# Token-layout projections of two mixers in chunks of 512 columns, both token tiles in turn

## Chip, cores and metric

The kernel runs as one program on one core of a Trainium2 chip. The metric is the device time of the execution in microseconds (us). The kernel before has a median of 2323.62 us over 3 runs, from 2319.12 to 2325.05. Engines are named as the profile names them: PE is the matrix engine (its weight loads are PEld), DVE, ACT and POOL are the vector, scalar and GpSimd engines, and SP is the one that issues most of the DMA transfers.

## What is computed

A sequence of 256 tokens with 1024 features, in float32, goes through two transformer blocks of two layers each. Both have a SwiGLU feed-forward network (FFN), a token mixer and a second FFN per layer. The change touches one product in each mixer: the projection of the tokens whose result is wanted with tokens on the partitions (`z = h @ w_in` and `proj = n @ w_in` below).

```
# first block, per layer
h = rms_norm(x, mix_norm[l])
z = h @ w_in[l]                      # 1024 -> 3200
rq, rk, rv, rg, mq, mk, mv, ca, cg = split(z)
rq, rk = rotary(rq), rotary(rk)      # all 64 dims of a head
y_ret  = retention(rq, rk, rv)       # 6 heads, decay instead of softmax
y_ret  = silu(rg) * y_ret * rsqrt(mean(y_ret * y_ret) + EPS)
mq, mk = rotary(mq), rotary(mk)      # 16 of 64 dims
y_moba = moba_attention(mq, mk, mv)  # 6 heads; at 256 tokens causal attention
y_conv = conv_module(ca, cg, ...)    # 31 taps over time, layer norm, silu
x = x + concat(y_ret, y_moba, y_conv) @ w_out[l]

# second block, per layer
proj = n @ w_in
nsa_q, nsa_kv, nsa_g, dil_qkv, fox_qkv, fox_f, merge_g = split(proj)
y_a = nsa_attention(...)             # 4 heads; compressed, selected, windowed
y_b = dilated_attention(...)         # 3 groups of 2 heads, 3 patterns
y_c = forgetting_attention(...)      # 6 heads
g_a, g_b, g_c = split(sigmoid(merge_g))
merged = g_a * (y_a @ br_nsa) + g_b * (y_b @ br_dil) + g_c * (y_c @ br_fox)
h = h + ga2 * (merged @ w_out)
```

## The kernel before

**Stages.** The program is one straight list: FFN, `mixer1`, FFN for each of the two layers of the first block, then FFN, `mixer2`, FFN for each of the second. Python code emits instructions; a scheduler that simulates a timeline then chooses, at compile time, the order in which each engine gets them, and moves independent matmuls into places where another chain waits. So each engine runs a fixed list, in order, and waits where a value is not there yet.

**Products in three terms.** Every large product splits its float32 operands in a high and a low part. `weights` (L117) loads the weights in parts of 1024 columns (`raw`, 4 buffers, by SP); ACT casts the high part `whi` (L132) and DVE subtracts the low part `wlo` (L133), 5 buffers each. `mm3` (L152) issues three matmuls for one k-slice of 128 features: high by high, high by low, low by high (L155 to L157).

**The token projections.** `tok_proj` (L365) makes a chunk of n columns for both tiles of 128 tokens. The normalized activations `hh` and `hl` stand still in PE and the weights move. Its result `tp` holds both token tiles, 2 x n float32, in one PSUM bank of the tag `mm`, which has three; the second tile comes after the whole first. Mixer 1 has 9 chunks of 256 columns (36 heads of 64: retention q, k, v, then moba q, k, v). Mixer 2 has 12: 210, 192 and ten of 256.

**Rotations and copies.** ACT copies a chunk from PSUM to `tk` (in mixer 1 once for each token tile, scaled by `rt`; in mixer 2 once for both tiles, L964). `rope` (L376) then rotates up to four heads: for each token tile four DVE instructions (L391 to L394), with the scratch tiles `ra` and `rb` in two buffers of four heads.

**Mixer 1.** `heads(i)` (L618) is one chunk with its copies and rotations. The order as written: chunks 0 to 2, the transposes of retention's q and k (`pairs`, tile `tpo`, L405), the two inputs of the convolution (`conv_in`, L541, matmuls into `pc`), chunks 3 and 4, retention, chunks 5 to 7, transposes for moba, chunk 8, moba's attention. Retention takes two heads at a time: scores `sp`, on DVE the product with the decay (`pts`, L656), the product with v (`acc`, L451 and L453), a copy, a square, and its mean `st` (L580). The convolution's 31 taps of the first 128 channels run on DVE (L562); those of the other 128 on ACT (L566) and POOL (L567).

**Mixer 2.** Chunk 1 gives the compressed branch its keys and values; its hidden layer `phd` (L866) multiplies with weights that a DMA brings into `w1`. Chunks 2 and 3 give NSA its windowed keys and its queries; `pcm` (L909) is the first score of the compressed branch. Then follow NSA's attention, the dilated branch (L961 to L994: scores `sp`, masks into `smd`, a softmax over 384 and 768 columns, transposed probabilities `pt`, products `acc`), the forgetting attention ("fox") and the output. Beside them `merge_gate` (L801) makes the gates: 24 `pg` per layer, which depend on the input alone, so that the scheduler has them as free work for PE; 7 of them come ahead of the mixer's input. A gate needs one of the three `mm` banks, one of 2 `z` and one of 10 `gate` buffers, and a `gate` buffer comes free when `branch` has used it. The first NSA `branch` needs NSA's result.

## Time and profile before

| | |
|---|---|
| median of 3 runs | 2323.62 us |
| lowest, highest | 2319.12, 2325.05 us |
| the profiled execution's own time | 2322.81 us |
| its span | 2321.0 us |
| mean granted clock of PE | 0.987 |
| PE busy | 2250.6 us, 97% |
| PEld busy | 2113.9 us, 91% |
| DVE busy | 1762.8 us, 76% |
| ACT busy | 1207.3 us, 52% |

The shares are means over the whole span. Matmuls overlap one another in PE's pipeline, so the time from the start of one to the start of the next, not the duration of one, is what a matmul costs in a dense stream. The table by stretch gives busy time and, in brackets, the number of instructions of each engine between two times; the clock there is the share of full speed granted to PE. A row of the timeline has the start, the duration of the instruction (or of several alike, with their count), the engine, the line of the program, and what it writes and reads; in brackets at the end the idle time of the engine before it and what released it.

### The profile page before, as it was taken

To read this page: it belongs to the slowest core of one execution; us is meant where nothing else is said; L and a number is where in the kernel's file an instruction comes from. 1 tells how busy PE (TensorE), PEld (TensorE's weight loads), DVE (VectorE), ACT (ScalarE), POOL (GpSimd) and SP (SyncE) were. 2 spreads that over 40 slices of the span, in tenths; PEclk is the share of its full clock that TensorE was granted. 3 is DMA by queue.
4 is the path that set the end of the run, shared out by engine and by line. 5 is a ranking of instruction groups with operands and counts; after the bars stand their busy time and mean duration, and the time that the engine had idled before them with its cause. 6 is when DMAs were issued, how large, how long until landed. Compare 5 with 4: busy or idle time off the path is not lost.

```text
span 2321.0 us, 43297 instructions
## 1 busy us (share of the span) xinstructions
PE 2250.6 (97%) x16976; PEld 2113.9 (91%) x16976; DVE 1762.8 (76%) x3255; ACT 1207.3 (52%) x1939; POOL 271.7 (12%) x286
## 2 busy tenths in 40 slices
PE   8999899989989899999999999999999999999998
PEld 8989779979988879998998989999999999899997
DVE  8988868887877968877776667777677666678764
ACT  5545565445435655455555555555455555556543
POOL 2210511111110402111001000200000010011000
PEclk9999999999999989999999999999999999999999
DMA  8887327887888426875456644455655665335553
GB/s 289 306 287 283 122 97 275 292 301 245 293 280 274 141 90 227 285 238 188 172 177 198 199 121 121 132 199 182 184 191 182 179 204 182 101 110 187 186 177 114
DMA packets 121148, 464.79 MB, mean 200 GB/s; under 512 B 13744, under 2 KB 15408, under 8 KB 111472
## 3 DMA queue, kind: packets, MB, share of 16 engines
q1 hardware_dynamic: 119216, 454.43, 59.4%
q0 software_dynamic: 1728, 7.60, 0.9%
q8 instruction: 133, 2.18, 0.4%
q14 instruction: 71, 0.58, 0.1%
HBM read 460.93 MB, written 1.05 MB: 199 GB/s over the span
## 4 chain that ended last, share of the span: by engine, by line
PE 65%; DMA 13%; DVE 11%; issue 8%; ACT 1%; POOL 1%; DVEq 0%; SPq 0%; ACTq 0%; POOLq 0%
PE acc L163 12%; DMA adar<-in_ada 10%; PE acc L164 6%; PE at L266 4%; PE at L264 4%; PE at L265 4%; PE mm L266 4%; PE mm L264 4%; PE mm L265 4%; DVE wlo L133 4%; DVE adar L760 3%; PE tp L156 2%; PE tp L155 2%; PE tp L157 2%; PE pg L266 2%
## 5 line engine op out<-in xcount | busy, mean ns | idle before, releaser
L132 ACT CAST whi<-raw 128x1024 fp32r<-128x1024 f32 (+2 forms) x739 | 753.4, 1023 | 697.5 <-PE acc L163 146.1
L133 DVE TENSOR_TENSOR wlo<-raw,whi 128x1024 fp32r<-128x1024 f32 (+2 forms) x739 | 889.7, 1208 | 226.3 <-ACT whi L132 223.7
L163 PE MATMUL acc<-hid,whi 128*128 128x512 f32 x1408 | 494.3, 395 | 7.7 <-DVE hid L147 5.8
L264 PE MATMUL mm<-hh,whi 128*128 128x256 f32 (+1 forms) x1408 | 398.3, 283 | 9.4 <-ACT whi L132 4.9
L266 PE MATMUL at<-hh,wlo 128*128 128x256 f32 (+1 forms) x1408 | 398.1, 283 | 9.1 <-DVE wlo L133 9.0
L266 PE MATMUL mm<-hh,wlo 128*128 128x256 f32 (+1 forms) x1408 | 398.9, 283 | 4.3 <-DVE wlo L133 4.3
L264 PE MATMUL at<-hh,whi 128*128 128x256 f32 (+1 forms) x1408 | 397.7, 282 | 1.6 <-DVE p L347 1.6
L164 PE MATMUL acc<-hid,wlo 128*128 128x256 f32 x1408 | 395.8, 281 | 3.2 <-DVE wlo L133 3.2
L265 PE MATMUL mm<-hl,whi 128*128 128x256 f32 x1408 | 395.6, 281 | 0.4 <-DVE hl L187 0.4
L265 PE MATMUL at<-hl,whi 128*128 128x256 f32 x1408 | 395.5, 281 | 0.0
L163 PEld LDWEIGHTS acc<-hid,whi 128*128 128x128 f32 x1408 | 266.3, 189 | 68.0 <-DVE hid L147 7.0
L266 PEld LDWEIGHTS at<-hh,wlo 128*128 128x128 f32 x1408 | 266.2, 189 | 11.0 <-DVE wlo L133 10.8
L264 PEld LDWEIGHTS mm<-hh,whi 128*128 128x128 f32 x1408 | 266.4, 189 | 10.1 <-ACT whi L132 4.9
L266 PEld LDWEIGHTS mm<-hh,wlo 128*128 128x128 f32 x1408 | 267.0, 190 | 5.5 <-DVE wlo L133 5.3
L164 PEld LDWEIGHTS acc<-hid,wlo 128*128 128x128 f32 x1408 | 266.6, 189 | 4.0 <-DVE wlo L133 3.9
L265 PEld LDWEIGHTS mm<-hl,whi 128*128 128x128 f32 x1408 | 267.6, 190 | 1.8 <-DVE hl L187 1.5
L264 PEld LDWEIGHTS at<-hh,whi 128*128 128x128 f32 x1408 | 265.7, 189 | 2.2 <-DVE p L347 2.0
L265 PEld LDWEIGHTS at<-hl,whi 128*128 128x128 f32 x1408 | 267.3, 190 | 0.2
L760 DVE SCALAR_TENSOR_TENSOR adar<-adar,cb 128x1024 f32<-128x1024 f32 x144 | 177.0, 1264 | 78.2 <-DMA adar<-in_ada 77.8
L200 POOL TENSOR_TENSOR ssq<-ssq,sq 128x256 f32<-128x256 f32 x78 | 74.2, 954 | 930.6 <-ACT sq L198 919.8
L346 POOL TENSOR_TENSOR s<-s,rs 128x256 f32<-128x256 f32 x88 | 103.6, 1178 | 445.4 <-ACT s L345 442.1
L146 ACT CAST hid<-p 128x256 fp32r<-128x256 f32 x176 | 71.5, 406 | 103.5 <-DVE p L347 92.9
(373 smaller groups left out, 3943.7 us busy)
## 6 DMA issues: line engine op xcount, KB each, us to landing
raw<-in_g_in SPq DMA_DIRECT2D x176, 512.0 KB, 4.4
raw<-in_f_in SPq DMA_DIRECT2D x175, 512.0 KB, 5.9
adar<-in_ada SPq DMA_DIRECT2D x72, 1024.0 KB, 5.9
raw<-in_m_tok SPq DMA_DIRECT2D x76, 512.0 KB, 4.1
raw<-in_f_out SPq DMA_DIRECT2D x64, 512.0 KB, 5.3
raw<-in_g_out SPq DMA_DIRECT2D x64, 512.0 KB, 3.5
raw<-in_m_merge SPq DMA_DIRECT2D x48, 512.0 KB, 3.6
raw<-in_m_out SPq DMA_DIRECT2D x32, 512.0 KB, 3.4
```

The source lines that it names most:

```text
L132: nc.scalar.copy(hi[:, c], raw[:, c])
L133: nc.vector.tensor_sub(lo[:, c], raw[:, c], hi[:, c].bitcast(F32))
L146: nc.scalar.copy(hi, src)
L155: mm(out, a[0], b[0], start=first, stop=False)
L163: mm(out, a[0], b, start=first, stop=False, skip_group_check=True)
L164: mm(out[:, 0], a[1], b[:, 1], start=False, stop=last, skip_group_check=True)
L200: nc.gpsimd.tensor_tensor(ssq, ssq, sq, op=ALU.add)
L264: mm(out, w[0], self.hh[:, k, 0:n], start=k == 0, stop=False)
L265: mm(out[:, 0:S], w[0], self.hl[:, k], start=False, stop=False)
L266: mm(out, w[1], self.hh[:, k, 0:n], start=False, stop=k == KD - 1)
L346: nc.gpsimd.tensor_tensor(s, s, rs, op=ALU.mult)
L760: nc.vector.scalar_tensor_tensor(raw[:, e], raw[:, e], 1.0, self.cb, op0=ALU.mult, op1=ALU.mult, accum_out=self.mod[:, l, j + e:j + e + 1])
```

## The change

**Chunks.** `tok_proj` with more than 256 columns now takes two tiles of 128 x n, one for each token tile, each a whole bank of `mm`; so a chunk holds two of the three banks. The loop over k is outside and the token tiles are inside, so that the three matmuls of one tile are followed by the three of the other with the same weights. Up to 256 columns it is as before; both forms return a list of two views.

**Mixer 1** has four chunks of 512 and one of 256. The order as written is: chunks 0 and 1, transposes, convolution inputs, chunk 2, retention, chunk 3, transposes, chunk 4, moba. `pairs` thus stands behind 1024 columns instead of 768. **Mixer 2** has chunks of 210, 448 (the former 192 and 256 together), three of 512, then 512 and 256 for fox's q and k; the former last chunk, half of fox's v, is in the third chunk of 512, and so is made ahead of the dilated branch. Copies go by token tile, rotations take up to eight heads, and their scratch tiles have eight heads and one buffer. The weights are laid out on the host to fit.

```diff
+RB = 1
...
-        out = self.ps.tile([128, 2, n], F32, name="tp", tag="mm", bufs=MM)
-        for t in range(2):
-            ts = slice(t * 128, (t + 1) * 128)
-            for k in range(KD):
-                self.mm3(out[:, t], (hh[:, k, ts], hl[:, k, ts]), w(k), k == 0, k == KD - 1)
+        if n <= 256:
+            out = self.ps.tile([128, 2, n], F32, name="tp", tag="mm", bufs=MM)
+            for t in range(2):
+                ts = slice(t * 128, (t + 1) * 128)
+                for k in range(KD):
+                    self.mm3(out[:, t], (hh[:, k, ts], hl[:, k, ts]), w(k), k == 0, k == KD - 1)
+            return [out[:, t] for t in range(2)]
+        out = [self.ps.tile([128, n], F32, name="tp", tag="mm", bufs=MM) for _ in range(2)]
+        for k in range(KD):
+            for t in range(2):
+                ts = slice(t * 128, (t + 1) * 128)
+                self.mm3(out[t], (hh[:, k, ts], hl[:, k, ts]), w(k), k == 0, k == KD - 1)
...
-            a = sc.tile([128, 4, w], F32, name=f"ra{w}", bufs=2)
-            b = sc.tile([128, 4, w], F32, name=f"rb{w}", bufs=2)
+            a = sc.tile([128, 8, w], F32, name=f"ra{w}", bufs=RB)
+            b = sc.tile([128, 8, w], F32, name=f"rb{w}", bufs=RB)
...
-                pz = self.tok_proj(wt[i], 256)
+                c = slice(i * 512, min(2304, i * 512 + 512))
+                pz = self.tok_proj(wt[:, c.start * KD:c.stop * KD], c.stop - c.start)
                 for t in range(2):
-                    nc.scalar.activation(tk[:, t, i * 256:(i + 1) * 256], pz[:, t], AF.Copy, scale=rt[:, t:t + 1])
+                    nc.scalar.activation(tk[:, t, c], pz[t], AF.Copy, scale=rt[:, t:t + 1])
                 for a, b, half, cc, ss in ((0, 12, 32, self.rcc, self.rss), (18, 30, 8, self.mcc, self.mss)):
-                    s0, s1 = max(a, i * 4), min(b, i * 4 + 4)
+                    s0, s1 = max(a, i * 8), min(b, i * 8 + 8)
...
-            for i in range(3):
+            for i in range(2):
                 heads(i)
             qr = pool.tile([128, 3, S], F32, name="qr")
             kr = pool.tile([128, 3, S], F32, name="kr")
             pairs(0, kr, qr)
             for i in range(2):
                 conv_in(i)
-            for i in range(3, 5):
-                heads(i)
+            heads(2)
...
-            for i in range(5, 8):
-                heads(i)
+            heads(3)
             qm = pool.tile([128, 3, S], F32, name="qm")
             km = pool.tile([128, 3, S], F32, name="km")
             pairs(18 * 64, km, qm)
-            heads(8)
+            heads(4)
...
-            nc.scalar.copy(nk, proj(210))
+            for t, p in enumerate(proj(210)):
+                nc.scalar.copy(nk[:, t], p)
...
-            nc.scalar.copy(n2, proj(192))
+            n3 = pool.tile([128, 2, 256], F32, name="n3", tag="kd")
+            for t, p in enumerate(proj(448)):
+                nc.scalar.copy(n2[:, t], p[:, 0:192])
+                nc.scalar.copy(n3[:, t], p[:, 192:448])
             self.rope(n2[:, :, 64:128], 8, cc, ss)
-            n3 = pool.tile([128, 2, 256], F32, name="n3", tag="kd")
-            nc.scalar.copy(n3, proj(256))
             self.rope(n3, 8, cc, ss)
...
-                nc.scalar.copy(tk[:, :, i * 256:(i + 1) * 256], proj(256))
-                s0, s1 = i * 4, min(12, i * 4 + 4)
+                for t, p in enumerate(proj(512)):
+                    nc.scalar.copy(tk[:, t, i * 512:(i + 1) * 512], p)
+                s0, s1 = i * 8, min(12, i * 8 + 8)
...
-            for i in range(3):
+            for i in range(2):
                 chunk(i)
             kd = pool.tile([128, 3, S], F32, name="kd")
             qd = pool.tile([128, 3, S], F32, name="qd", tag="qa")
             for g in range(3):
                 nc.scalar.copy(qd[:, g], self.tpose(tk, g * 128))
                 nc.vector.tensor_copy(kd[:, g], self.tpose(tk, 384 + g * 128))
-            for i in range(3, 5):
-                chunk(i)
+            chunk(2)
...
-            for i in range(3):
-                pz = proj(256)
+            for i in range(2):
+                pz = proj(512 if i == 0 else 256)
                 for t in range(2):
-                    zz = pz[:, t].rearrange("p (n c) -> p n c", c=64)
+                    zz = pz[t].rearrange("p (n c) -> p n c", c=64)
                     if i == 0:
-                        nc.scalar.copy(fq[:, t, 0:4, 0:64], zz)
-                    elif i == 1:
-                        nc.scalar.copy(fq[:, t, 4:6, 0:64], zz[:, 0:2])
-                        nc.vector.tensor_copy(fk[:, t, 0:2, 0:64], zz[:, 2:4])
+                        nc.scalar.copy(fq[:, t, :, 0:64], zz[:, 0:6])
+                        nc.vector.tensor_copy(fk[:, t, 0:2, 0:64], zz[:, 6:8])
                     else:
                         nc.scalar.copy(fk[:, t, 2:6, 0:64], zz)
-            chunk(5)
```

The order of the instructions changes at more places than the diff shows. Three of them follow; the number in a tile's name is the scheduler's own, lines of the changed kernel stand some 1 to 9 higher than before.

The first is PE's list in mixer 1 of layer 0, where the convolution's input `pc` begins. `tp` is a token chunk and `tpo` a transposed pair of heads. Before:

```order
L155 MATMUL tp_2585<-whi_2580,hh_1805 128x256
L156 MATMUL tp_2585<-wlo_2581,hh_1805 128x256
L157 MATMUL tp_2585<-whi_2580,hl_1806 128x256
L405 MATMUL tpo_2650<-cst_87,tk_2411 128x128 x2
L264 MATMUL pc_2686<-hh_1805,whi_2675 128x256
```

In the changed kernel:

```order
L156 MATMUL tp_2536<-whi_2530,hh_1805 128x512
L157 MATMUL tp_2536<-wlo_2531,hh_1805 128x512
L158 MATMUL tp_2536<-whi_2530,hl_1806 128x512
L413 MATMUL tpo_2601<-cst_87,tk_2411 128x128 x2
L413 MATMUL tpo_2605<-cst_87,tk_2411 128x128 x2
L413 MATMUL tpo_2609<-cst_87,tk_2411 128x128 x2
L265 MATMUL pc_2637<-hh_1805,whi_2626 128x256
```

Before, `pc` stood behind three chunks of 256 columns; now it stands behind two of 512.

The second is PE's list at the third head pair of retention, in the same mixer: `sp` are its scores, `acc` the product with v, `st` the means of squares. Before, a chunk `tp` fills the place behind the scores:

```order
L155 MATMUL tp_3313<-whi_3302,hh_1805 128x256
L580 MATMUL st_3003<-cst_87,sq_3001 128x2 x2
L653 MATMUL sp_3018<-qr_2648,kr_2649 128x256
L654 MATMUL sp_3018<-qr_2648,kr_2649 128x128
L653 MATMUL sp_3023<-qr_2648,kr_2649 128x256
L654 MATMUL sp_3023<-qr_2648,kr_2649 128x128
L156 MATMUL tp_3313<-wlo_3303,hh_1805 128x256
L157 MATMUL tp_3313<-whi_3302,hl_1806 128x256
```

In the changed kernel:

```order
L610 MATMUL st_3354<-cy0_2692,cst_87 128x256
L588 MATMUL st_2904<-cst_87,sq_2902 128x2 x2
L661 MATMUL sp_2919<-qr_2599,kr_2600 128x256
L662 MATMUL sp_2919<-qr_2599,kr_2600 128x128
L661 MATMUL sp_2924<-qr_2599,kr_2600 128x256
L662 MATMUL sp_2924<-qr_2599,kr_2600 128x128
L459 MATMUL acc_2918<-pts_2922,tk_2411 64x256
L459 MATMUL acc_2918<-pts_2927,tk_2411 64x256
L461 MATMUL acc_2918<-pts_2922,tk_2411 64x128
L461 MATMUL acc_2918<-pts_2927,tk_2411 64x128
L588 MATMUL st_2937<-cst_87,sq_2935 128x2 x2
L413 MATMUL tpo_3041<-cst_87,tk_2411 128x128 x2
```

No chunk stands between the scores and their product any more; the chain runs from `st` to the first `tpo` of moba with nothing between.

The third is PE's list in the dilated branch of mixer 2, layer 0: `sp` are scores, `pt` transposed probabilities, `pg` the matmuls of a merge gate, `acc_15295` the branch's product with v, and `acc_15601` the first matmuls of the NSA `branch`. Before:

```order
L431 MATMUL sp_15918<-kd_15756,qd_15757 128x128
L432 MATMUL sp_15918<-kd_15756,qd_15757 128x256
L264 MATMUL pg_16646<-hh_14095,whi_16641 128x258
L265 MATMUL pg_16646<-hl_14096,whi_16641 128x256
L431 MATMUL sp_15932<-kd_15756,qd_15757 128x128
L432 MATMUL sp_15932<-kd_15756,qd_15757 128x256
L266 MATMUL pg_16646<-hh_14095,wlo_16642 128x258
```

In the changed kernel:

```order
L439 MATMUL sp_15321<-kd_15193,qd_15194 128x128
L440 MATMUL sp_15321<-kd_15193,qd_15194 128x256
L439 MATMUL sp_15326<-kd_15193,qd_15194 128x128
L440 MATMUL sp_15326<-kd_15193,qd_15194 128x256
L439 MATMUL sp_15331<-kd_15193,qd_15194 128x128
L440 MATMUL sp_15331<-kd_15193,qd_15194 128x256
L450 MATMUL pt_15344<-cst_87,smd_15296 128x128 x3
L450 MATMUL pt_15350<-cst_87,smd_15320 128x128
L450 MATMUL pt_15360<-cst_87,smd_15296 128x128 x3
L459 MATMUL acc_15295<-pts_15348,tk_15016 64x256
L450 MATMUL pt_15366<-cst_87,smd_15320 128x128
L156 MATMUL acc_15601<-yh_14195,whi_15558 128x256
```

Merge gates stood between the scores; now the six pairs of scores and the first transposes follow one another (three of the pairs are shown), and the next other work is the NSA branch. The eight gates that came there stand earlier in the list, in the compressed branch and NSA: `pcm` is now behind all seven token chunks, before behind eight of twelve.

## Rows read from the trace of the kernel before

**Rows 1.** The page, busy time of each engine: us, share of span, instructions.

```profile
PE 2250.6 (97%) x16976; PEld 2113.9 (91%) x16976; DVE 1762.8 (76%) x3255; ACT 1207.3 (52%) x1939; POOL 271.7 (12%) x286
```

**Rows 2.** Stretches: length, busy (count) of PE, PEld, DVE, ACT, POOL; clock; DMA.

```profile
240.00:275.00 35.00, 26.98 (x204) 23.61 (x202) 34.65 (x55) 23.95 (x47) 27.79 (x29) 0.90 0.29 101
1294.00:1356.00 62.00, 61.37 (x541) 59.49 (x540) 38.05 (x117) 32.08 (x52) 1.06 (x2) 1.00 0.54 170
1391.00:1427.00 36.00, 35.97 (x263) 30.52 (x261) 22.51 (x61) 17.13 (x30) 0.00 (x0) 1.00 0.36 104
```

**Rows 3.** Waits of PE: what waited for what, us, times, longest.

```profile
PE acc L451 <- DVE pts L656: 16.0, 4, 6.9
```

**Rows 4.** Timeline of PE in mixer 1, layer 0: start, duration, instruction, idle before.

```profile
264.48 0.28 PE L155 MATMUL tp<-whi,hh 128*128 128x256 f32 x1
271.69 1.12 PE L451 MATMUL acc<-pts,tk 128*64 128x256 f32 x2 [6.93 <-DVE pts L656]
...
289.33 0.85 PE L405 MATMUL tpo<-cst,tk 128*128 128x128 f32 x6
```

**Rows 5.** Timeline of PE: mixer 1's chunks in layer 1; an FFN's second half.

```profile
777.31 0.28 PE L155 MATMUL tp<-whi,hh 128*128 128x256 f32 x1
...
788.55 0.28 PE L157 MATMUL tp<-whi,hl 128*128 128x256 f32 x1
...
151.11 0.39 PE L163 MATMUL acc<-hid,whi 128*128 128x512 f32 x1
151.34 0.28 PE L164 MATMUL acc<-hid,wlo 128*128 128x256 f32 x1
```

**Rows 6.** Tile `tp`, ACT's copies (ns min/median/max); timeline of PE at `phd`.

```profile
  L964 ACT COPY tk<-tp x12: 587/588/589, 1316.8 to 2000.1; 128x512 f32<-128x512 f32 x12
...
1328.06 0.39 PE L866 MATMUL phd<-w,blk 128*15 128x128 f32 x2 [0.63 <-DMA w<-in_cw]
```

**Rows 7.** Timeline of POOL and DVE in the middle of mixer 1, layer 0.

```profile
241.77 29.98 POOL L567 TENSOR_TENSOR cy<-cy,ct 128x256 f32<-128x256 f32 x29 [1.94 <-ACT ct L566]
...
241.49 1.21 DVE L133 TENSOR_TENSOR wlo<-raw,whi 128x1024 fp32r<-128x1024 f32 x1
242.62 3.60 DVE L562 SCALAR_TENSOR_TENSOR cy<-u,vec,cy 128x256 f32<-128x256 f32 x4
246.15 1.76 DVE L133 TENSOR_TENSOR wlo<-raw,whi 128x1024 fp32r<-128x1024 f32 x1
247.83 0.95 DVE L562 SCALAR_TENSOR_TENSOR cy<-u,vec,cy 128x256 f32<-128x256 f32 x1
...
253.02 0.55 DVE L656 TENSOR_TENSOR pts<-sp,dec 128x384 f32<-128x384 f32 x1
...
253.82 0.73 DVE L391 TENSOR_TENSOR ra<-tk,mcc 128x32 f32<-128x32 f32 x1
```

**Rows 8.** Timeline of DVE, ACT and PE in mixer 2's dilated branch, layer 0.

```profile
1401.33 0.29 DVE L984 SCALAR_TENSOR_TENSOR smd<-sp,dil 128x128 f32<-128x128 f32 x1 [0.52 <-PE sp L432]
...
1401.87 1.40 DVE L413 TENSOR_REDUCE nm<-smd 128x1 f32<-128x384 f32 x2
...
1406.00 0.94 DVE L426 TENSOR_SCALAR smd<-smd,nm 128x384 f32<-128x384 f32 x2
...
1403.31 0.94 ACT L415 ACTIVATE smd<-smd,nm 128x768 f32<-128x768 f32 x1
1404.15 0.19 ACT L415 ACTIVATION_READ_ACCUMULATOR smd<-smd,nm 128x1 f32 x1
...
1402.71 0.48 PE L431 MATMUL sp<-kd,qd 64*128 64x128 f32 x2
...
1403.56 0.39 PE L265 MATMUL pg<-hl,whi 128*128 128x256 f32 x1
```

**Rows 9.** Stretches of mixer 1, layer 0, columns as in rows 2.

```profile
272.00:276.00 4.00, 4.00 (x18) 2.33 (x17) 3.93 (x13) 0.96 (x3) 0.03 (x1) 0.61 0.30 102
...
300.00:306.00 6.00, 6.00 (x19) 2.76 (x17) 3.15 (x17) 4.32 (x15) 0.00 (x0) 0.50 0.00 0
```

More of the change, by code (lines that the diff above doesn't have):

```diff
@@ L1154, in layout @@
     ca, cg = w[..., 2688:2944], w[..., 2944:3200]
-    r["m1_tok"] = cols(np.concatenate([rq, rk, rv, mq, mk, mv], -1), 256)
+    w = np.concatenate([rq, rk, rv, mq, mk, mv], -1)
+    r["m1_tok"] = np.concatenate([cols(w[..., :2048], 512)[:, i] for i in range(4)] + [cols(w[..., 2048:], 256)[:, 0]],
+                                 -1)
     ft = cols(np.concatenate([ca[..., :128], cg[..., :128], ca[..., 128:], cg[..., 128:], rg,
@@ L1167, in layout @@
     rest = np.concatenate([dl, fx[..., 768:]], -1)
-    groups = [np.concatenate([ff, gates, kc, vc, ks], -1), np.concatenate([vs, kw, vw], -1), q]
-    groups += [rest[..., i * 256:(i + 1) * 256] for i in range(5)]
-    groups += [fx[..., i * 256:(i + 1) * 256] for i in range(3)] + [rest[..., 1280:]]
+    groups = [np.concatenate([ff, gates, kc, vc, ks], -1), np.concatenate([vs, kw, vw, q], -1)]
+    groups += [rest[..., i * 512:(i + 1) * 512] for i in range(3)]
+    groups += [fx[..., :512], fx[..., 512:768]]
     r["m2_tok"] = np.concatenate([cols(g, g.shape[-1])[:, 0] for g in groups], -1)
```

## The prediction

> **What bounds the kernel now.** I read the page's busy shares first [rows 1]: TensorE (PE) is busy 97% of 2321.0 us, VectorE (DVE) 76%, ScalarE (ACT) 52%. These are averages, so next the table by stretch [rows 2]. In mixer 2 of layer 0, from 1294 to 1356 and from 1391 to 1427 us, PE is busy 61.37 of 62 us (token chunks) and 35.97 of 36 (dilated branch): PE's own work is the time there. In mixer 1, from 240 to 275 us, PE is busy only 26.98 of 35 us and DVE 34.65: there DVE's list is the time. Then the waits [rows 3] and the place of the longest [rows 4]: `acc` waits for the `pts` tiles that DVE makes, 16.0 us in four waits; the one in layer 0 keeps PE from 264.48 to 271.69, and layer 1 has its like. So what a change does to PE counts everywhere but in mixer 1's middle, and what it does to DVE counts there.
>
> **Part 1, fewer and wider matmuls.** A chunk is 2 token tiles x 8 k x 3 terms = 48 matmuls, whatever its width. Mixer 1 goes from 9 chunks to 5 and mixer 2 from 12 to 7, so 9 x 48 x 2 layers = 864 matmuls go, and as many become twice as wide (one chunk 448). Spacing counts, not the duration of one [rows 5]: 95 steps of 256 columns take 788.55 - 777.31 = 11.24 us, 118.3 ns each; a matmul of 512 columns in the FFN's second half is followed after 0.23 us (151.11 to 151.34). So a pair becomes 2 x 118.3 - 230 = 6.6 ns cheaper. For mixer 2's 480 pairs that is -3.2 us, all on the path; mixer 1's 384 go into part 3. The Trainium skill ("TensorE: Matmul & The Clock Gate", section "Back-to-back issue gap") states a sustained 131 ns per matmul at 512 columns; that would be about 118 + 118 - 131 = 105 ns a pair, by estimate 90 us in all. The trace disagrees: its 512-wide matmuls, in a dense stream, stand 230 ns apart.
>
> **Part 2, banks, copies, rotations.** A 512-wide chunk takes two of the three `mm` banks, so the next chunk's second tile waits until a copy has emptied a bank. In the new order PE runs 18 to 20 matmuls of the next chunk's first tile ahead (20 x 0.23 = 4.6 us), and a 512-wide copy on ACT takes 0.59 us [rows 6]: covered, 0; without that cover it would be about 0.6 us for each of 20 changes of chunk. Rotations lose 64 DVE instructions in all; in mixer 2 PE's work hides them, in mixer 1 they are in part 3. One scratch buffer instead of two costs nothing, since DVE takes the two tiles in turn anyway. In mixer 2 `phd` waits 0.63 us for its weights [rows 6]; between its two groups now lie 35 wide matmuls (8.0 us) instead of 50 narrow ones (5.9 us), so the wait goes: -1.2 us in two layers.
>
> **Part 3, mixer 1.** The convolution's input `pc` now comes behind two 512-chunks instead of three 256-chunks: 96 x 0.230 = 22.1 us against 144 x 0.1183 = 17.0 us, so all its taps begin 5.0 us later (241.8 to about 247 us; one `wlo` more stands before them). From then GpSimd (POOL) runs 29 taps in 29.98 us [rows 7], and meanwhile DVE's work on SBUF tiles is slow: a tap 0.88 us (four in 246.15 - 242.62), a `wlo` 1.76 instead of 1.21, the first instruction of a rotation 0.73. In the new DVE order those 30 us hold 18 taps (15.8), 6 `wlo` (10.1 at a spacing of 1.68), one rotation of two tiles (3.0) and the first pair of `pts` (0.55 each): 30.0 us. Behind it come 4.3 us more to the second pair, so that is ready near 281.6 us, against 271.7 before. PE arrives at it near 271 us: the wait grows from 7 to about 9 or 10 us. Against that, 256 columns of chunk work are gone from behind it. What follows is a chain without filler: `acc` 0.5, copy and square 0.8 with two hops, `st`, scores 1.7, `pts` 1.2, `acc` 1.1, copy and square 1.2: about 290.5 us at the first `tpo`, which was at 289.33 [rows 4]. I take +1 us a layer, +2 in all. Its ends are -3 (the 16 rotation instructions that leave the 30 us at about 0.33 us each, 5 us, less 2 for what I have already counted) and +5 (the later start in full).
>
> **Part 4, mixer 2's dilated branch, the largest term.** Before, PE fills this branch's softmax chain with matmuls of the merge gates (`pg`), and the compress and NSA chain ahead of it with token chunks: `pcm` stands behind 8 of 12 chunks. In the new order `pcm` stands behind all chunks, so eight gates are spent before and during NSA. No more can be: 10 `gate` buffers, 2 `z` and 3 banks hold 15 gates, the 7 early ones and these 8. In the dilated branch six score pairs and then `pt` stand in a row with nothing between. The chain from the first score, t = 0, by [rows 8]: a pair of `sp` takes 0.85 us on PE (1402.71 to 1403.56) and the third is ready at 2.7. DVE: two `smd` 0.5 (3.2), the maximum over 384 0.5, one `smd` of the other half 0.2, the maximum over 768 0.9 (4.8). ACT: the exponential 0.94 and its sum 0.19 (5.95). DVE: reciprocal 0.2, the other half's two maxima 1.3, the two scalings 0.94 (8.5). PE has done its scores at 5.1 and starts `pt` at 8.6: 3.5 us idle. Another 0.45 follow at the other half's first scaling, and 0.7 before the first score, at copies of `tpo`: 4.7 us. Then the clock: behind the 7 us wait in mixer 1 PE ran 4 us at 0.61 of its clock, and where small matmuls stand between waits it ran at 0.50, its lower level of 1.2 GHz [rows 9]. Half speed doubles the six pairs (+2.5 us up to the third, which holds the chain) and adds about 1.6 us behind. Ends: +3 us (half of the 4.7 found filled after all, by branch matmuls) and +11 (all of it, and ACT's six copies late). The likeliest is nearer to the second kind, since 295 to 306 us in mixer 1 is the same kind of work with the same lack of filler: +7.5 us a layer, +15 in all.
>
> **Sum**, against the profiled execution of 2322.8 us (span 2321.0; the runs' median of 2323.6 is 0.8 above it): -3.2 - 1.2 + 2 + 15 = +12.6, so about 2335 us. Differences under 0.3%, 7 us, are not told from no change.
>
> **Rivals.**
> A. Faster: DVE's list in mixer 1 shortens and sets the end there. Its 16 rotation instructions fewer at 0.33 us give -5.3 us a layer, if the later tap start is absorbed, and the hole of part 4 costs its low end: 2322.8 - 4.4 - 10.6 + 6 = 2314 us. For it: DVE is busy 34.65 of 35 us there. Against it: POOL's 30 us begin 5 us later and no row shows slack behind. It decides if the second `pts` pair comes before about 274 us.
> B. No change: the hole is the warm 4.7 us only and mixer 1 is even: 2322.8 - 4.4 + 9.4 = 2328 us.
> C. Worse: clock and copies take both upper ends: 2322.8 - 4.4 + 10 + 22 = 2350 us. For it speak the 0.50 in [rows 9].
> D. A wide matmul costs PE hardly more than a narrow one: 864 x 118 ns = 102 us less, 2221 us, as long as nothing else binds. The row of 230 ns is against it. It is what the skill's sustained figure would mean.
> That the change does nothing is out: the new order has 875 PE rows fewer, and shows widths of 512.
>
> **How the numbers follow.** Forecast 0.53, A 0.13, B 0.25, C 0.07, D 0.02. Forecast and C are slower by over 0.3% (0.60), B is the same (0.25), A and D are faster (0.15). The range goes from just above A, 2316, to C's 2350; A, D and what lies beyond C stay out, and B is in.
>
> **What would show it.** Right: spacing of 230 ns in the token chunks; in the dilated branch PE idle for 3 us or more between the last `sp` and the first `pt`, at a lower clock behind it; the wait for the second `pts` pair at 9 us or more; `phd` without its wait. Wrong: PE full through the dilated branch, or a first `tpo` of mixer 1 several us before 289 us.

## The result, and the profile after

The changed kernel takes 2340.02 us (median of 6 runs, 2331.31 to 2344.04) against 2322.53 us before (6 runs). The ratio is 1.0078, with a 95% interval from 1.0055 to 1.0100: slower by 17.5 us, where 12.6 were forecast. The profiled execution has a span of 2337.4 us, at a mean clock of 0.976 (before 0.987).

The page of the changed kernel, busy time of each engine, answers to [rows 1]:

```profile
span 2337.4 us, 41491 instructions
PE 2255.5 (96%) x16112; PEld 2083.6 (89%) x16112; DVE 1761.1 (75%) x3191; ACT 1206.7 (52%) x1925; POOL 267.4 (11%) x286
```

PE has 864 matmuls fewer, as counted, and yet is busy 4.9 us longer. Where that comes from is seen when the span is cut at marks that both kernels have. Each mixer is taken here from the first matmul of the norm ahead of it (`pss`) to the first `pss` behind its out projection. The table by stretch, columns as in [rows 2], gives mixer 1 of both layers and mixer 2 of both layers. Before:

```profile
205.23:349.85 144.62, 133.78 (x1005) 119.51 (x1004) 114.47 (x252) 87.20 (x179) 39.34 (x40) 0.94 0.41 138
746.84:891.50 144.66, 134.15 (x1006) 120.35 (x1005) 114.23 (x251) 86.74 (x178) 39.30 (x40) 0.93 0.39 131
1272.98:1513.02 240.04, 238.12 (x1889) 217.92 (x1888) 170.61 (x430) 132.73 (x258) 19.70 (x27) 1.00 0.48 146
1885.19:2125.22 240.03, 238.14 (x1889) 217.91 (x1887) 170.61 (x430) 132.70 (x258) 19.70 (x27) 1.00 0.47 146
```

After:

```profile
207.32:361.90 154.58, 140.14 (x813) 116.19 (x812) 114.28 (x227) 86.45 (x170) 38.95 (x40) 0.88 0.39 126
759.01:909.16 150.15, 136.77 (x815) 113.29 (x814) 113.76 (x227) 86.45 (x170) 39.42 (x40) 0.91 0.40 126
1290.22:1529.16 238.94, 234.68 (x1649) 205.46 (x1648) 170.13 (x419) 132.77 (x258) 18.44 (x27) 0.99 0.47 146
1901.23:2141.35 240.12, 233.80 (x1646) 205.35 (x1645) 170.05 (x420) 132.39 (x258) 17.21 (x27) 0.99 0.47 145
```

Mixer 1 is 9.96 and 5.49 us longer, mixer 2 is 1.10 us shorter and 0.09 longer, and the rest of the span differs by 2.0 us. So nearly the whole loss sits in mixer 1, where the prediction had put 2 us of it; that the total came near is luck, since it is the sum of two terms that were wrong in opposite directions. In mixer 1 the length is PE's busy time and its idle time. Idle time grew by 3.6 and 2.9 us (154.58 - 140.14 = 14.44 against 10.84; 13.38 against 10.51). Busy time grew by 6.4 and 2.6 us, with 192 matmuls fewer, at a clock of 0.88 and 0.91 instead of 0.94 and 0.93.

The waits of PE, as in [rows 3]; the rows are the four that bear on the change:

```profile
PE acc L459 <- DVE pts L664: 17.8, 4, 8.3
PE pt L450 <- DVE smd L434: 7.7, 4, 3.7
PE pt L450 <- ACT sm L432: 5.7, 4, 2.5
PE st L588 <- ACT sq L670: 3.7, 4, 1.2
```

The second and the fourth are new; the first was 16.0 us, and the third was this one before:

```profile
PE pt L442 <- ACT sm L424: 4.6, 4, 1.7
```

In mixer 1, then, the waits grew by 3.3 us a layer: 0.9 for `pts`, 0.6 for `sm` and, the most, 1.9 for `sq`. A token chunk stood between `st` and its neighbours in PE's list before; now `st` and its neighbours follow one another. There is no row for `phd` any more.

The timeline of PE in mixer 1, layer 0, at the places of [rows 4]:

```profile
273.07 0.28 PE L158 MATMUL tp<-whi,hl 128*128 128x256 f32 x1
281.61 0.69 PE L459 MATMUL acc<-pts,tk 128*64 128x256 f32 x1 [8.26 <-DVE pts L664]
...
295.97 0.67 PE L413 MATMUL tpo<-cst,tk 128*128 128x128 f32 x2
```

And the table by stretch behind it, to the end of retention (two rows) and in moba's attention, to be read for PE's busy time and count and for the clock, the third number from the end. After:

```profile
288.00:292.00 4.00, 2.38 (x13) 1.74 (x12) 2.21 (x4) 1.26 (x3) 0.00 (x0) 0.74 0.55 185
292.00:296.00 4.00, 2.92 (x13) 1.99 (x13) 0.58 (x2) 1.09 (x3) 0.00 (x0) 0.50 0.16 65
...
305.00:307.00 2.00, 0.77 (x3) 0.34 (x3) 2.00 (x16) 1.82 (x7) 0.00 (x0) 1.00 0.00 0
307.00:312.00 5.00, 4.80 (x14) 2.65 (x15) 2.72 (x18) 4.77 (x18) 0.00 (x0) 0.50 0.02 3
312.00:317.00 5.00, 5.00 (x18) 2.78 (x16) 1.76 (x5) 3.33 (x11) 0.00 (x0) 0.50 0.00 0
317.00:322.00 5.00, 5.00 (x18) 3.26 (x16) 3.17 (x8) 2.33 (x6) 0.00 (x0) 0.50 0.00 0
322.00:324.00 2.00, 2.00 (x9) 1.36 (x9) 0.00 (x0) 0.00 (x0) 0.00 (x0) 0.50 0.00 0
324.00:326.00 2.00, 2.00 (x15) 1.42 (x13) 0.42 (x1) 1.11 (x3) 0.00 (x0) 0.98 0.00 0
```

Before, the same place:

```profile
298.00:300.00 2.00, 1.27 (x4) 1.06 (x5) 1.97 (x20) 2.00 (x8) 0.00 (x0) 0.75 0.00 0
300.00:304.00 4.00, 4.00 (x11) 1.70 (x10) 2.03 (x14) 3.07 (x11) 0.00 (x0) 0.50 0.00 0
304.00:308.00 4.00, 4.00 (x16) 2.09 (x15) 1.71 (x6) 3.26 (x11) 0.00 (x0) 0.50 0.00 0
308.00:310.00 2.00, 2.00 (x11) 0.98 (x9) 0.00 (x0) 1.02 (x3) 0.00 (x0) 0.69 0.00 0
310.00:312.00 2.00, 2.00 (x13) 1.57 (x12) 1.22 (x4) 0.39 (x2) 0.00 (x0) 1.00 0.00 0
```

In both kernels PE waits for moba's softmax (at most 1.7 us at a time before, 2.5 after), and its clock then falls to the lower level, 1.2 GHz. Before, it was back at full speed after some 10 us, ahead of the gate matmuls `pg`, which begin at 311. After, it stays low from 307 to 324 us, some 17 us, and the first gate matmuls, from 318 on, run at half speed too.

Mixer 2's dilated branch, layer 0, is as forecast. PE's timeline from the last scores to the first transposes:

```profile
1429.59 0.59 PE L440 MATMUL sp<-kd,qd 64*128 64x256 f32 x2
1433.88 1.22 PE L450 MATMUL pt<-cst,smd 128*128 128x128 f32 x3 [3.69 <-DVE smd L434]
```

The table by stretch over it:

```profile
1430.00:1434.00 4.00, 0.31 (x2) 0.12 (x1) 4.00 (x11) 2.62 (x7) 0.00 (x0) 0.92 0.01 2
1434.00:1438.00 4.00, 3.77 (x12) 1.99 (x13) 1.47 (x4) 1.04 (x3) 0.00 (x0) 0.50 0.00 0
1438.00:1442.00 4.00, 4.00 (x25) 3.37 (x23) 1.40 (x5) 1.72 (x5) 0.00 (x0) 0.72 0.00 0
```

PE waits 3.69 us for the scaled probabilities, with DVE busy all the time, and then runs at half clock from 1434 to some 1440 us. That the mixer is none the longer means that something gave more back than forecast: the token chunks and, as the runs below show, the single scratch buffer.

The wide matmuls, as in [rows 5]; one of 512 columns follows the other after 0.23 us:

```profile
1348.93 0.39 PE L156 MATMUL tp<-whi,hn 128*128 128x512 f32 x1
1349.16 0.40 PE L157 MATMUL tp<-wlo,hn 128*128 128x512 f32 x1
```

### The profile page after: what moved, and what is told of

Read it like the earlier page. It is cut to its first block, busy times and chain, and to the rows that moved or that the text cites. A ratio compares the mean times of both kernels' runs of the same rounds, so it can differ in the third digit from the quotient of the medians.

```text
span 2337.4 us, 41491 instructions
## 1 busy us (share of the span) xinstructions
PE 2255.5 (96%) x16112; PEld 2083.6 (89%) x16112; DVE 1761.1 (75%) x3191; ACT 1206.7 (52%) x1925; POOL 267.4 (11%) x286
## 4 chain that ended last, share of the span: by engine, by line
PE 78%; DVE 9%; DMA 7%; issue 4%; ACT 1%; POOL 1%; SPq 0%; DVEq 0%; ACTq 0%; POOLq 0%
PE acc L164 12%; PE acc L165 6%; DMA adar<-in_ada 6%; PE at L267 6%; PE at L265 5%; PE mm L267 5%; PE mm L265 5%; PE at L266 5%; PE mm L266 5%; DVE wlo L134 3%; PE tp L156 3%; PE tp L158 3%; PE tp L157 3%; PE pg L265 2%; PE pg L267 2%
## 5 line engine op out<-in xcount | busy, mean ns | idle before, releaser
L133 ACT CAST whi<-raw 128x1024 fp32r<-128x1024 f32 (+3 forms) x739 | 753.3, 1023 | 720.5 <-PE acc L164 148.0
L134 DVE TENSOR_TENSOR wlo<-raw,whi 128x1024 fp32r<-128x1024 f32 (+3 forms) x739 | 892.6, 1212 | 229.0 <-ACT whi L133 226.1
```

The source lines that it names most:

```text
L133: nc.scalar.copy(hi[:, c], raw[:, c])
L134: nc.vector.tensor_sub(lo[:, c], raw[:, c], hi[:, c].bitcast(F32))
```

## The experiments

Twelve kernels were run, each beside the kernel before. In the texts that were written ahead of the runs, mixer 1 is counted to the first matmul of its out projection, `oa`. In some of these kernels `oa` starts among moba's last matmuls, so the lengths given below are those from `pss` to `pss`, as above, unless the text says otherwise.

### Which mixer loses the time

Mixer 1 as in the changed kernel, mixer 2 with twelve chunks as before.

> Mixer 1 as in the changed kernel, mixer 2 with its twelve chunks as before. Theory after the first look at the two traces (the time is lost in mixer 1): mixer 1, counted from the last norm matmul `pss` to the first `oa`, stays near 128 and 124 us in the two layers instead of 118.4, and the whole takes 14 to 16 us more than before, 2336 to 2339 us. The prediction's split (mixer 1 +1 us a layer, the rest in mixer 2) would give 2324 to 2326 us.

Measured: 2334.74 us, ratio 1.0051 (1.0034 to 1.0068). The two rows are mixer 1 in both layers:

```profile
204.52:354.33 149.81, 135.50 (x813) 112.25 (x812) 114.40 (x227) 87.18 (x171) 39.55 (x40) 0.92 0.39 129
750.12:900.92 150.80, 136.59 (x816) 113.03 (x815) 113.67 (x227) 86.36 (x170) 39.42 (x40) 0.91 0.40 127
```

The other way round, mixer 2 as changed, mixer 1 with nine chunks of 256.

> Mixer 2 as in the changed kernel, mixer 1 with its nine chunks of 256 as before. Theory (lost in mixer 1): mixer 2 keeps its hole in the dilated branch (3.7 us of waiting ahead of the first `pt` and a lower clock behind it), but its token chunks cost 5 to 6 us a layer less, so the whole is within 3 us of before: 2320 to 2326 us. The prediction's split (+5.3 us a layer net in mixer 2) would give 2331 to 2335 us.

Measured: 2323.47 us, ratio 1.0006 (0.9993 to 1.0020); mixer 2 took 239.48 and 240.96 us, mixer 1 144.93 and 144.17. So mixer 1 carries the loss and mixer 2 is even. In the first run mixer 1 was longer by 5.2 and 6.1 us. The changed kernel's layer 0 was longer by 10.0 with the same order of instructions in that mixer: the clock fell there once more, already at 290 us, at the end of retention. So about half of those 10 us are not there in each execution. The profiled execution of the first run is also one of its fastest, 2325.59 us against the median of 2334.74, so that its trace does not show where the whole 13 us of the median lie.

The first of these runs held a surprise: mixer 2, with its chunks as before, took 236.83 and 236.59 us instead of 240.0. Both runs keep the changed kernel's single scratch buffer, which a later run takes up by itself.

### The late start of the taps

The prediction's reason for mixer 1 was that the convolution's taps begin 5 us later, behind two wide chunks. This edit makes them late in the kernel before, without any wide chunk:

```diff
-            for i in range(3):
+            for i in range(4):
                 heads(i)
...
-            for i in range(3, 5):
+            for i in range(4, 5):
                 heads(i)
```

> The kernel before with one edit: the convolution's inputs are written behind four chunks of 256 instead of three, so the taps start 48 narrow matmuls later, 48 x 0.118 = 5.7 us; no chunk is wide. Theory (the late start of the taps sets mixer 1): the second pair of `pts` comes 5 to 8 us later than its 66.4 us after `pss`, and mixer 1 takes 3 to 8 us more in each layer, 2329 to 2339 us in all. Rival (what costs is the wide chunks, as filler that is missing behind retention, or the single scratch buffer): no more than 1 us a layer, 2322 to 2326 us.

Measured: 2318.72 us, ratio 0.9984 (0.9970 to 0.9998). Mixer 1 was shorter, 143.31 and 141.28 us. The taps of POOL did begin 5.6 us later, but PE's wait for the second pair of `pts` fell:

```profile
273.60 0.69 PE L451 MATMUL acc<-pts,tk 128*64 128x256 f32 x1 [5.50 <-DVE pts L656]
```

That is 63.1 us behind `pss`, against 66.5 before. The new order put the pair earlier in DVE's list, so that it was made while POOL's taps still ran. So a late start of the taps does not by itself make the pair late or the mixer longer. The test from the other side, the changed kernel with narrow chunks ahead of the convolution:

```diff
+M1W = [256, 256, 256, 512, 512, 256, 256]
...
-                c = slice(i * 512, min(2304, i * 512 + 512))
+                c = slice(sum(M1W[:i]), sum(M1W[:i + 1]))
...
-            for i in range(2):
+            for i in range(3):
                 heads(i)
```

> The changed kernel with mixer 1's chunks as 3 x 256, 2 x 512, 2 x 256: the convolution's input stands behind three chunks of 256 again, and the retention's v, moba's q and most of its k are made in wide chunks. Theory (late start of the taps): the second pair of `pts` is back at 66 to 68 us after `pss`, mixer 1 at 117 to 121 us in both layers, the whole at 2319 to 2328 us. Rival (the wide chunks behind the convolution, or the single scratch buffer, lose the time): mixer 1 stays at 123 to 128 us, the whole at 2334 to 2341 us.

Measured: 2331.86 us, ratio 1.0041 (1.0027 to 1.0054). The taps began early again (37.6 us behind the first token matmul instead of 42.2), and the second pair of `pts` came early with them, 69.3 us behind `pss` instead of 74.3:

```profile
276.29 1.12 PE L460 MATMUL acc<-pts,tk 128*64 128x256 f32 x2 [8.56 <-DVE pts L666]
```

PE waited no less for it, and mixer 1 took 149.22 and 149.77 us, at a clock of 0.91. So the pair came earlier when the taps did, but the length of the mixer did not follow; the whole lies between the two ranges that were expected. Two wide chunks behind the convolution were enough to lose 5 us a layer. Moba's first transpose came 1.1 us later than before, and the stage from there to the first `oa` was 3.5 us longer (37.6 against 34.1, means of both layers).

### Rotations, and the order of the token tiles

Two other parts of the change could have been to blame. The first run undoes the rotations: four heads at a time, two scratch buffers, in the kernel with mixer 1 alone changed.

> Mixer 1 alone changed, as in the run with mixer 1 alone, but the rotations take four heads at a time again, with two scratch buffers. Theory (the wide chunks themselves, by the order they bring, lose the time): mixer 1 stays at 122 to 126 us a layer from the first token matmul to the first `oa`, against 118.2 before, the whole at 2331 to 2337 us. Rival (rotations of eight heads on a single scratch buffer lose it): mixer 1 is back at 117 to 120 us, the whole at 2320 to 2326 us.

Measured: 2334.32 us, ratio 1.0052 (1.0036 to 1.0069), the same as with eight heads. Mixer 1 in both layers:

```profile
203.38:358.09 154.71, 139.42 (x814) 115.70 (x812) 116.54 (x251) 87.50 (x171) 38.87 (x40) 0.88 0.38 125
753.53:905.08 151.55, 136.33 (x815) 112.80 (x814) 116.36 (x251) 87.55 (x172) 39.15 (x40) 0.91 0.39 127
```

Nothing is won back: PE's wait for the second pair is 9.34 us instead of 8.30, and layer 0 has the clock of 0.88 of the changed kernel again. Mixer 2, with two scratch buffers, is at 239.05 and 239.13 us. The second changes the order of the loops in a wide chunk:

```diff
-        for k in range(KD):
-            for t in range(2):
+        for t in range(2):
+            for k in range(KD):
```

> The changed kernel with one edit: in a wide chunk the first token tile is made whole before the second (the loop over tiles outside, over k inside). Theory (the two tiles in turn cost nothing themselves): the same within 3 us, 2336 to 2343 us, mixer 1 at 122 to 128 us a layer. Rival (because both tiles of a chunk are done only at its end, copies, rotations and what follows come late): the first tile is done 24 x 0.23 = 5.5 us earlier, and mixer 1 takes 3 to 6 us a layer less, 2326 to 2333 us in all.

Measured: 2338.54 us, ratio 1.0074 (1.0058 to 1.0090), mixer 1 150.74 and 151.06 us. Neither is to blame for the loss. But the second is instructive, because the long wait for `pts` was shorter there. Its timeline of PE in layer 0:

```profile
276.42 0.58 PE L157 MATMUL tp<-wlo,hh 128*128 128x256 f32 x1 [5.26 <-DVE wlo L134]
...
282.38 0.65 PE L459 MATMUL acc<-pts,tk 128*64 128x256 f32 x2 [1.02 <-DVE pts L664]
```

The pair came no earlier, 75.4 us behind `pss`; most of the wait has moved ahead, to a chunk that waits for its `wlo`. Mixer 1 of both layers as a stretch:

```profile
207.00:357.74 150.74, 139.52 (x814) 116.74 (x813) 114.40 (x227) 85.86 (x170) 39.56 (x40) 0.89 0.40 128
756.01:907.07 151.06, 140.49 (x816) 117.33 (x814) 113.81 (x227) 85.67 (x170) 39.27 (x40) 0.89 0.39 125
```

Against the changed kernel, PE is idle 3.2 and 2.8 us less. In layer 0, where the changed kernel's profiled execution had the extra fall of the clock, the mixer is 3.8 us shorter. In layer 1 PE is busy 3.7 us longer, at a clock of 0.89 instead of 0.91: there the lower clock takes what the shorter idle time gives.

### Gate matmuls ahead of moba

New theory: mixer 1 loses time because moba's stage runs longer at half clock, with dense work, the gates, inside that stretch. This edit moves two of the three retention gates out of it, in the kernel with mixer 1 alone changed. They depend on the mixer's input alone.

```diff
             pr = [probs(0)]
+            for g in range(2):
+                gate(g)
...
             for g in range(3):
-                w = self.weights(wf[2 + g // 2][:, (g % 2) * 1024:(g % 2 + 1) * 1024], 1024)
-                pg = ps.tile([128, S], F32, name="pg", tag="mm", bufs=MM)
-                for k in range(KD):
-                    self.mm_in(pg, w(k), k, S)
-                z = sb.tile([128, S], F32, name="z", bufs=2)
-                nc.vector.tensor_tensor(z, pg, rs, op=ALU.mult)
+                if g == 2:
+                    gate(g)
+                z = zs[g]
```

`gate(g)` holds the lines taken out and keeps the result in `zs`.

> Mixer 1 alone changed, and the matmuls of two of the three retention gates (`pg`, 48 matmuls, 5.7 us at full clock) written ahead of moba's attention instead of behind it. Theory (behind its waits moba's stage runs at half clock, 17 us of it against 10 before, and that is what the wide chunks cost there): with 48 matmuls taken out of that stretch, the stage from moba's first transpose to the first `oa` falls from 37.3 us to 29 to 32 us, and mixer 1 to 118 to 122 us; the whole at 2322 to 2331 us. Rival (the chain of DVE and ACT sets that stage, PE's clock is only seen there): the stage shrinks by less than 3 us, and mixer 1 grows to 125 to 129 us, since 5.7 us are added ahead; 2336 to 2344 us.

Measured: 2307.07 us, ratio 0.9934 (0.9918 to 0.9950), faster than both kernels. The first two rows are mixer 1 in both layers, the others moba's stage in layer 0:

```profile
205.10:348.08 142.98, 129.82 (x817) 109.81 (x816) 114.14 (x227) 86.57 (x171) 39.06 (x40) 0.94 0.41 134
738.94:881.52 142.58, 129.81 (x818) 109.29 (x816) 114.34 (x227) 85.90 (x171) 39.10 (x40) 0.95 0.41 134
...
305.00:307.00 2.00, 1.43 (x8) 1.12 (x9) 1.27 (x13) 2.00 (x8) 0.00 (x0) 0.50 0.00 0
307.00:311.00 4.00, 3.85 (x18) 2.15 (x15) 2.31 (x7) 2.73 (x10) 0.00 (x0) 0.50 0.00 0
311.00:313.00 2.00, 2.00 (x9) 1.15 (x8) 0.75 (x3) 2.00 (x9) 0.00 (x0) 0.86 0.00 0
313.00:315.00 2.00, 2.00 (x19) 1.80 (x20) 1.81 (x6) 1.53 (x5) 0.00 (x0) 1.00 0.00 0
```

The same matmuls keep PE busy 5.7 and 6.8 us less than with mixer 1 alone changed (129.8 against 135.5 and 136.6), and it is idle only 1.2 and 1.4 us less. The stretch at half clock is some 7 us instead of 17. By the mean clocks of the whole mixer (0.92 and 0.91 without the edit, 0.94 and 0.95 with it; 0.08 of 150 us against 0.06 of 143 in layer 0) the clock gives back at most some 3 us in layer 0 and 6 in layer 1; in layer 0 part of the gain in busy time stays unexplained. By the first `oa` the effect was larger than expected, 112.9 and 112.7 us where 118 to 122 stood. The fair mark, the end of the out projection, gives 6.8 and 8.2 us. The medians differ by 27 us, the two profiled executions by 21: 15 of these lie in mixer 1, and 6 in the stages between the mixers, which none of these edits touch. Where the rest of the 27 lies no trace shows.

The same edit in the whole changed kernel.

> The changed kernel, both mixers in wide chunks, with two of the three retention gates written ahead of moba's attention. Theory (what the change loses is the stretch at half clock in mixer 1, and mixer 2 is even): mixer 1 as in the earlier run with gates ahead, 111 to 115 us from the first token matmul to the first `oa` instead of 123 to 128; mixer 2 at 186 to 188 us; the whole at 2308 to 2316 us. Rival (the two mixers' losses are not separate): 2320 to 2334 us.

Measured: 2309.25 us, ratio 0.9964 (0.9949 to 0.9980). Mixer 1 took 142.55 and 143.67 us, by the first `oa` 112.8 and 113.8 as expected, and mixer 2 238.65 and 239.48. And in the kernel before, together with the scratch buffer of the next section.

> All chunks of 256 as before, one scratch buffer of eight heads, and two of the three retention gates written ahead of moba's attention. Theory (the stretch at half clock behind moba's waits costs the kernel before too, 10 us of it, and goes the same way): mixer 1 falls from 118 to 110 to 114 us, the whole to 2300 to 2309 us. Rival (narrow chunks left enough between the waits; the gates add 5.7 us ahead and give little back): mixer 1 at 116 to 120 us, the whole at 2312 to 2320 us.

Measured: 2311.13 us, ratio 0.9963 (0.9948 to 0.9978). Mixer 1 took 145.22 and 144.02 us, against 144.99 and 144.16 without the gates ahead: nothing. By the first `oa` it took 115.6 and 115.0 us, between the two ranges, and so does the whole. The theory overreached here, and its rival had the mechanism: with narrow chunks the gates already stood where the clock was back up, and moving them gains nothing. So they repair what the wide chunks break, and a little more: 142.8 us a layer with wide chunks and gates ahead, against 144.6 with narrow ones. What they give is busy time; PE's idle time stays 2.3 us a layer above that of the kernel before. All three gates ahead:

> Mixer 1 in wide chunks, mixer 2 as before, and all three retention gates written ahead of moba's attention (72 matmuls, 8.5 us at full clock), the third in a buffer of its own. With two of them ahead, mixer 1 from its first norm matmul to the end of its out projection takes 142.8 and 142.4 us, against 149.6 and 150.6 with none. Theory (gate work at half clock is what can be moved out): the third gate brings no more than 2 us a layer on top, mixer 1 at 140 to 143 us, the whole at 2300 to 2309 us. Rival (with nothing dense left between moba's small matmuls the stage stays longer at half clock): mixer 1 at 144 to 148 us, the whole at 2309 to 2318 us.

Measured: 2311.25 us, ratio 0.9952 (0.9936 to 0.9968); mixer 1 took 146.60 and 143.29 us. The third gate gains nothing: layer 0 and the whole are in the rival's range, layer 1 between the two ranges. Two are the better number.

### The scratch buffer alone

The kernel before with one edit, `ra` and `rb` with eight heads and one buffer instead of four heads and two.

> The kernel before with one edit: the rotations' scratch tiles are one buffer of eight heads instead of two of four. Theory from the run with mixer 1 alone (there mixer 2, with chunks as before, took 184.6 us a layer instead of 187.0, and the scratch was the one thing it shared with the change): mixer 2 takes 184 to 185.5 us here too, the whole is 3 to 6 us below before, 2316 to 2319 us. Rival (that gain came from elsewhere): no difference, 2320 to 2324 us.

Measured: 2315.36 us, ratio 0.9976 (0.9964 to 0.9988). Mixer 2 in both layers:

```profile
1266.53:1503.25 236.72, 235.46 (x1890) 216.80 (x1889) 170.69 (x427) 131.34 (x257) 18.08 (x27) 1.00 0.48 147
1875.32:2111.85 236.53, 235.30 (x1889) 216.71 (x1888) 170.50 (x427) 131.21 (x257) 18.42 (x27) 1.00 0.48 147
```

The same matmuls keep PE busy 2.7 us less a layer, at full clock in both kernels. The edit leaves the work alone and changes the scheduler's order. Counted in the trace, PE changes 95 times instead of 115 between three-term matmuls and the small float32 ones, and its time without waits, from `pss` to the first `oa`, falls from 207.1 to 204.6 us: about 0.13 us for each change of kind. That the changes of kind are the cause is worked out from these counts; no run measured one by itself.

This changes the reading of mixer 2. Against narrow chunks with the same single scratch buffer (236.72 and 236.53 us), mixer 2 in wide chunks (239.48 and 240.96 with mixer 1 narrow) is 2.8 and 4.4 us longer. It is even with the kernel before only because the change brings the scratch buffer along.

### Filler in the dilated branch

Mixed widths in mixer 2, so that other matmuls stand among the dilated scores again; mixer 1 narrow, with the taps late and two gates ahead.

```diff
-            for i in range(2):
-                chunk(i)
+            chunk(0, 256)
+            chunk(256, 256)
+            chunk(512, 256)
...
-            chunk(2)
+            chunk(768, 512)
...
-            for i in range(2):
-                pz = proj(512 if i == 0 else 256)
+            for i in range(3):
+                pz = proj(256)
...
+            chunk(1280, 256)
```

> Mixer 1 in nine chunks of 256, the convolution's input behind four of them, two retention gates ahead of moba. Mixer 2 in chunks of 210, 448, three of 256, one of 512 (dilated v and half of fox's v), three of 256 for fox and one of 256 behind them; one scratch buffer of eight heads in both. In this order 57 other matmuls stand among the dilated branch's scores, as in the kernel before (58), and none in the changed kernel. Theory (the hole ahead of the first `pt` is missing filler, while the merged 448 chunk and a wide one save time): PE does not wait there, mixer 2 at 182 to 185 us, the whole at 2294 to 2304 us. Rival (the hole comes with wide chunks, whatever stands between): a wait of 2 us or more ahead of `pt`, mixer 2 at 186 us or more, the whole at 2304 to 2312 us.

Measured: 2308.03 us, ratio 0.9958 (0.9939 to 0.9977). No wait of `pt` for `smd` was left in PE's list of waits, and from its first token matmul to the first `oa` mixer 2 took 184.5 us in both layers (186.6 and 187.6 in the changed kernel). So the hole goes when the filler is back, as the prediction had it; the edit brings the filler by making chunks narrow again, and no run tells the two apart. Nor do the mixed widths win anything: narrow chunks with one scratch buffer also took 184.5 us by the first `oa`. The whole is in the rival's range, not the theory's; mixer 1, at 144.36 and 143.23 us, is no shorter for its gates ahead.

## Why the prediction was right, and where it was not

**Direction and size.** Forecast 2335 us, slower, range 2316 to 2350; measured 2340.0. The sum of the terms was +12.6, against +16.6 for the two profiled executions and +17.5 for the medians. The sum came near by luck: two of its terms are wrong, in opposite directions, and a third effect, the scratch buffer's, was not in it.

**Part 1.** A wide matmul in a dense stream takes 0.23 us, as read from [rows 5]. The Trainium skill ("TensorE: Matmul & The Clock Gate", section "Back-to-back issue gap") states a sustained 131 ns at 512 columns. Here the 738 steps between two 512-wide chunk matmuls of the changed kernel have a median of 232 ns, so the trace disagrees and rival D is out. The term itself was too small. Mixer 2's token matmuls, each counted to the start of PE's next instruction and without waits, went from 72.2 to 67.2 us a layer: -5.0, where 1.6 were forecast. The step that failed costed every pair as two of 118.3 ns in a clean stream. But the chunks of 192 and 210 columns stood 112 ns apart, hardly less than 256 columns do, so that joining 192 and 256 in 448 (205 ns) saved 25 ns a pair. And before, 29 of a layer's 576 token matmuls had a small float32 matmul behind them, at 0.17 us a step, after only 12 of 336. The token matmul that follows such a small one is slow as well: 27 took 0.20 to 0.23 us before, 11 some 0.1 us above the others after. Of the -5.0, 1.1 are the scratch buffer's: with it alone the same narrow chunks take 71.1 us.

**Part 2.** No token chunk waits for a bank, the scratch buffer does not slow mixer 1, and the wait of `phd` is gone, -1.2 us: right. That one scratch buffer costs nothing was right in sign only: by its own it made the kernel 0.24% faster, and mixer 2 3.3 and 3.5 us a layer shorter, by the order that it brings. The forecast for mixer 2 put this at nothing.

**Part 3, the step that failed.** Up to the wait the numbers nearly held: the second `pts` pair was forecast near 281.6 us and came at 281.61 (7.8 us later than before by mixer 1's own start, where 9.9 were forecast); PE waited 8.26 us, where 9 to 10 were. The reason given for it, the later start of the taps, holds for the pair in part (with the taps early again it came 5 us earlier), but not for the mixer's length: late taps alone made the kernel no slower, and early ones did not bring the loss back. How much of DVE's list stands ahead of the pair may be what counts; that was not tested by itself. Behind the wait, the chain to the first `tpo` was worked out at full clock, 290.5 us; it came at 295.97 (3.4 us late by mixer 1's own start), while PE ran at the lower clock and waited for `sq` four times in the two layers, 3.7 us. And everything behind the first `tpo` was held to be unchanged. It took 39.2 and 36.8 us to the first `oa` instead of 34.3 and 33.9. The prediction had the clock in its account for mixer 2, with the 0.50 of [rows 9] taken from this very stage, and did not ask what a longer gap ahead would do to the stage itself. The term was +1 us a layer; it measured +5.2 and +6.1 with mixer 1 alone changed, and +10.0 and +5.5 in the profiled changed kernel.

**Part 4.** The mechanism was right: six pairs of scores in a row, a hole of 3.69 us (3.5 forecast), half clock behind it. The size was a little less than forecast. From its first token matmul to the first `oa` mixer 2 took 186.6 and 187.6 us, against 187.0 before; with -5.0 for the chunks and -0.6 for `phd`, that leaves +5.2 and +6.2 us for all the rest, where +7.5 stood. The forecast left out that the dilated scores in a row also take less, 3.9 us of steps instead of 5.1. Against the right base, narrow chunks with one scratch buffer, mixer 2 is 2.8 and 4.4 us longer, which is nearer to the forecast's net 5.3 than its evenness with the kernel before suggests.

**Rivals.** A (faster by DVE's list) is out: PE's wait for `pts` grew. B had both mixers nearly even, and came nearest on mixer 2 alone, for a reason that it did not have (the scratch buffer). C was the worse clock; it came, but in mixer 1.

## What to carry to other kernels

When a change takes independent work out of a latency-bound stage, or joins it in larger pieces, cost the stage behind the gap at both clock levels: here PE's idle time grew by 3 to 4 us a layer, and its busy time, at a lower clock, by another 2 to 6. Where PE stands at half clock between small dependent matmuls, look for dense work inside that stretch and move it ahead: two gates moved gave 27 us of 2334 by the medians, 21 by the profiled executions, of which 15 lie in mixer 1. In narrow chunks, where the gates already ran at full clock, the same move gave mixer 1 nothing. And with a scheduler that fixes the order, an edit meant to be neutral (one scratch buffer, -0.24%) can hide part of what a change costs (+0.78% with it), so each part of a change is worth a run of its own.

## What was not expected of the hardware

- Less idle time need not make a stage shorter. With the token tiles one after the other PE was idle 2.8 us less in mixer 1 of layer 1 than in the changed kernel, but busy 3.7 us more, at a mean clock of 0.89 instead of 0.91, and the mixer took 151.06 us instead of 150.15.
- A change between token matmuls and small float32 ones can cost on both sides. In mixer 2 of the kernel before, layer 0, 15 of the 30 steps from a token matmul to a matmul of another product, and 27 of the 28 steps of the token matmuls right behind such a place, took 0.2 us or more instead of 0.12.
- Token matmuls below 256 columns gain little: steps of 112 ns at 192 and at 210 columns, 118 at 256, 205 at 448, 232 at 512 (medians of the steps from one token matmul to the next).
- What stays open: the stages between the mixers, which are the same code in all kernels, add up to 1551.7 us in the profile of before, 1553.6 in that of the changed kernel, 1543.4 with mixer 1 alone and gates ahead, and 1558.7 with late taps. Most of it is in the FFNs of the first block. The stretch ahead of the first mixer, where PE's list is the same in all kernels, alone took from 202.0 to 210.5 us in the profiled executions, so that one execution can differ from another by as much. No run was made to settle it, and so of the fastest kernel's gain only what lies in the mixers is explained.
